# Score operands of a dilated attention kept in two orders, output halves joined by DMA, transposes ahead of scores

## Chip, cores and metric

The kernel runs on one core of a Trainium2 chip. The metric is the device time of one execution in microseconds (us). Three runs of the kernel before took 2604.08, 2596.65 and 2601.12 us, median 2601.12.

## What is computed

One encoder layer on 2048 positions of width 1024. The input is normalised and projected once; half of the mixing width goes to attention (8 heads of 64), half to a gated unit that works in chunks of 128 positions. Attention runs three branches per head, with (window, dilation) of (128, 1), (512, 4) and (2048, 16): each query sees 64 keys on either side at that dilation, and itself.

```python
def dilated_window_branch(q, k, v, rel_bias, window, dil):
    # query at p attends to keys p + dil*j for |j| <= window // (2*dil)
    ...
    s = jnp.einsum('brnqhd,brnkhd->brnhqk', qb, kw).astype(jnp.float32)
    s = s + bias.transpose(2, 0, 1)
    s = jnp.where(valid[:, None], s, NEG_INF)
    m = jnp.max(s, axis=-1, keepdims=True)
    p = jnp.exp(s - m)
    den = jnp.sum(p, axis=-1, keepdims=True)
    o = jnp.einsum('brnhqk,brnkhd->brnqhd', (p / den).astype(v.dtype), vw)
    lse = (m + jnp.log(den))[..., 0].transpose(0, 1, 2, 4, 3)
```

The branches are summed per position with weights in proportion to their softmax denominators. Attention and gated unit go through one output projection, then a feed-forward of width 4096 with squared ReLU follows.

## The kernel before

Every float32 number that TensorE multiplies is split into a high and a low part of a shorter format, and a product is made of three matmuls (high-high, high-low, low-high). The program has three stages.

**The input stage** (0 to 412 us of the trace) normalises and transposes blocks of 512 positions (`prep_all`) and projects them. `do_v` writes values by position to DRAM (`c.vd`), `do_qk` queries and keys by channel (`c.qd`, `c.kd`: high part in [0], low part in [1], 128 channels = two heads each). Four PSUM banks are filled by 96 matmuls; ScalarE and VectorE split each bank into `e2`, and two DMAs of SyncE's queue write the two halves.

**The attention stage** (412 to 1037) goes through 8 heads in 12 steps each: steps 0 to 3 of a head are branch 2 (dilation 16), 4 to 7 branch 1 (dilation 4), 8 to 11 branch 0. A step handles 512 queries; branch 2 has one half step with four blocks of 128 keys, the others have two half steps with two blocks of 192 or 256 keys. Four phases of different heads' steps run together. In step s the program issues the scores and maxima of step s, the exponentials (ScalarE) of s-14, the transposes of s-15, and the values and the gather of s-16. So the values of branch 0 run in steps 0 to 3 of the next head but one.

- `scores`: queries are the stationary operand of 128 columns, with high and low part of the query on the upper and lower 64 partitions of `qs`; keys move, `kl` (low) first, then `ks` (high). For branches 1 and 2 the operands are read from the natural order with a stride of 4 or 16 numbers (`cols`).
- `maxima`: VectorE adds the bias, writes the sum to a tile `p` of a pool of 25 and the negative maximum to `nm`.
- `transposes`, `upper`, `lower`: TensorE turns p into a PSUM tile `t`, ScalarE takes the high part `th`, VectorE the low part `tl`.
- `values`: TensorE, into `o`, a PSUM pool of one buffer. `gather`: branch 2 opens `acc`, branch 1 adds, branch 0 makes `av` (from the pool of p), whose lower 64 partitions (L612) hold the part of the low values. A DMA (L615) brings those to `lo`, GpSimd adds (L619) and writes the head's output `od` (L620).
- `filler`: between these, matmuls of the gated unit (`f`, three at a time, and its transposes), spread by a plan over all steps; the splits `xh` and `xl` that they need are GpSimd's.

TensorE and ScalarE keep the order in which the program is written (`in_order`). The order on VectorE, GpSimd and SyncE is the scheduler's. The loads of the next head are issued in steps 3 to 8 and the values at steps 2, 6 and 10; a paced load waits for the TensorE instruction ahead of it in the program.

**The output stage** (1037 to 1182) and the feed-forward (to the end) are not touched by the change.

## Time and profile before

| | before |
|---|---|
| runs, us | 2604.08, 2596.65, 2601.12 |
| the profiled execution, us | 2600.37 |
| its span, us | 2598.4 |
| TensorE busy | 2451.3 us (94%) |
| VectorE / ScalarE / GpSimd busy | 1053.6 / 942.9 / 431.3 us |
| DMA | 296.13 MB, mean 114 GB/s |

The span is what the trace covers; the rest of the execution lies around it. The clock of TensorE over the span is 0.976 of full. Over the whole program TensorE is the busiest engine, but its share differs by stage: the table of stretches shows where it idles and where its granted clock falls. In rows of the time line the first number is the start, the second the duration, and the bracket tells how long the engine was idle before and what released it.

### The profile page before, as it was taken

How to read it: one execution, taken by the hardware profiler on the slowest of the kernel's cores; microseconds unless marked ns; L12 is line 12 of the kernel's file. 1: busy time of each engine (PE TensorE's matmuls, PEld its weight loads, DVE VectorE, ACT ScalarE, POOL GpSimd, SP SyncE). 2: the span in 40 equal slices, each digit the busy share in tenths (PEclk: the TensorE clock that was granted, in tenths of full speed). 3: DMA queues.
4: the chain of work that ended last, by engine and by line, in shares of the span. 5: the costliest groups of instructions: out<-in, count | busy, mean ns of one | idle time of the engine just before them, and what ended most of it. 6: DMA issues, size and time to landing. Idle time of an engine off the chain costs nothing.

```text
span 2598.4 us, 31362 instructions
## 1 busy us (share of the span) xinstructions
PE 2451.3 (94%) x11591; PEld 2053.8 (79%) x11591; DVE 1053.6 (41%) x2246; ACT 942.9 (36%) x2053; POOL 431.3 (17%) x489
## 2 busy tenths in 40 slices
PE   7999999988898897778999999999999999999998
PEld 6787888877787786557888888888788888888887
DVE  5534523555655554444133223322641332333235
ACT  4424322455665674434322212221533222122212
POOL 4103102322221122322001100110210011001101
PEclk9999999999999998889999999999999999999999
DMA  7644555755665545765121112111431111111113
GB/s 271 217 140 174 171 166 170 197 143 147 172 160 142 138 136 160 212 208 176 33 65 49 49 33 65 49 45 37 157 118 43 55 49 49 41 57 49 49 40 123
DMA packets 208765, 296.13 MB, mean 114 GB/s; under 512 B 37089, under 2 KB 112356, under 8 KB 205540
## 3 DMA queue, kind: packets, MB, share of 16 engines
q1 hardware_dynamic: 202436, 273.15, 35.8%
q10 hardware_dynamic: 4640, 16.79, 1.6%
q0 software_dynamic: 1536, 4.20, 0.6%
q8 instruction: 91, 1.49, 0.2%
q14 instruction: 62, 0.51, 0.1%
HBM read 216.04 MB, written 78.55 MB: 113 GB/s over the span
## 4 chain that ended last, share of the span: by engine, by line
PE 75%; DMA 10%; DVE 6%; issue 4%; POOL 3%; ACT 2%; SPq 1%; POOLq 0%; DVEq 0%; ACTq 0%
PE f L84 11%; PE f L85 11%; PE f L86 11%; PE g L86 8%; PE g L84 8%; PE g L85 8%; PE mm L85 3%; PE mm L86 3%; PE mm L84 3%; DMA fr<-rd 2%; PE s L492 2%; PE s L493 2%; PE t L569 2%; DVE p L505 1%; DMA lo<-av 1%
## 5 line engine op out<-in xcount | busy, mean ns | idle before, releaser
L84 PE MATMUL f<-hl,wh 128*128 128x512 f32 x1024 | 399.2, 390 | 4.7 <-ACT wh L56 4.7
L85 PE MATMUL f<-hh,wl 128*128 128x512 f32 x1024 | 399.2, 390 | 2.9 <-DVE wl L57 2.9
L84 PE MATMUL g<-wl,fh 128*128 128x512 f32 x1024 | 399.0, 390 | 0.0
L86 PE MATMUL f<-hh,wh 128*128 128x512 f32 x1024 | 398.8, 389 | 0.0
L85 PE MATMUL g<-wh,fl 128*128 128x512 f32 x1024 | 398.6, 389 | 0.0
L86 PE MATMUL g<-wh,fh 128*128 128x512 f32 x1024 | 398.5, 389 | 0.0
L56 ACT ACTIVATE wh<-wraw,gain 128x512 fp32r<-128x512 f32 x200 | 143.3, 724 | 502.0 <-PE g L86 423.2
L955 POOL TENSOR_TENSOR sq<-sq 128x512 f32<-128x512 f32 x128 | 132.1, 1052 | 1160.6 <-ACT sq L954 1160.6
L57 DVE SCALAR_TENSOR_TENSOR wl<-wraw,gain,wh 128x512 fp32r<-128x512 f32 x200 | 155.6, 785 | 271.7 <-ACT wh L56 269.1
L60 DVE TENSOR_TENSOR fl<-sq,fh 128x512 fp32r<-128x512 f32 x128 | 99.3, 776 | 394.4 <-ACT fh L59 385.4
L84 PEld LDWEIGHTS f<-hl,wh 128*128 128x128 f32 x1024 | 192.6, 188 | 45.2 <-ACT wh L56 5.1
L85 PEld LDWEIGHTS f<-hh,wl 128*128 128x128 f32 x1024 | 192.6, 188 | 43.3 <-DVE wl L57 3.4
L86 PEld LDWEIGHTS f<-hh,wh 128*128 128x128 f32 x1024 | 192.6, 188 | 40.0
L86 PEld LDWEIGHTS g<-wh,fh 128*128 128x128 f32 x1024 | 192.2, 188 | 39.9
L85 PEld LDWEIGHTS g<-wh,fl 128*128 128x128 f32 x1024 | 192.2, 188 | 39.7
L84 PEld LDWEIGHTS g<-wl,fh 128*128 128x128 f32 x1024 | 192.2, 188 | 39.7
L982 DVE TENSOR_TENSOR acc<-g,acc 128x512 f32<-128x512 f32 x192 | 127.2, 688 | 165.0 <-PE g L86 165.0
L492 PE MATMUL s<-kl,qs 128*128 128x256 f32 (+2 forms) x384 | 144.9, 385 | 48.1 <-DVE nm L505 44.8
L954 ACT ACTIVATE sq<-f 128x512 f32<-128x512 f32 x128 | 74.8, 597 | 289.9 <-PE f L86 282.7
L558 ACT ACTIVATE p<-p,m 128x256 f32<-128x256 f32 (+2 forms) x384 | 173.3, 456 | 4.0 <-DVE m L530 4.0
L505 DVE CUSTOM_DVE_ANT_0 p<-s,bias 128x256 f32<-128x256 f32 (+2 forms) x384 | 120.2, 353 | 127.9 <-PE t L569 71.9
L60 DVE TENSOR_TENSOR wl<-wraw,wh 128x512 fp32r<-128x512 f32 x144 | 100.2, 697 | 172.9 <-ACT wh L59 171.5
(150 smaller groups left out, 4197.6 us busy)
## 6 DMA issues: line engine op xcount, KB each, us to landing
wraw<-in_w_ff_dram SPq DMA_DIRECT2D x256, 256.0 KB, 2.8
wraw<-in_w_in_dram SPq DMA_DIRECT2D x72, 256.0 KB, 2.9
xt<-in_x_dram SPq DMA_DIRECT2D x32, 512.0 KB, 6.5
v<-vd SPq DMA_DIRECT2D x40, 256.0 KB, 6.2
v<-vd SPq DMA_DIRECT2D x8, 1088.0 KB, 7.6
hd<-ht ACTq DMA_DIRECT2D x16, 512.0 KB, 3.7
vd<-vt SPq DMA_DIRECT2D x16, 512.0 KB, 3.1
qd<-e SPq DMA_DIRECT2D x32, 256.0 KB, 2.8
```

Of the source, the lines that this page charges most:

```text
L56: nc.scalar.activation(hi, src, AF.Copy, scale=scale)
L57: nc.vector.scalar_tensor_tensor(lo, src, scale, f32(hi), ALU.mult, ALU.subtract)
L60: nc.vector.tensor_tensor(lo, src, f32(hi), ALU.subtract)
L84: nc.tensor.matmul(out, lhsT=lh, rhs=rl, start=start, stop=False)
L85: nc.tensor.matmul(out, lhsT=ll, rhs=rh, start=False, stop=False)
L86: nc.tensor.matmul(out, lhsT=lh, rhs=rh, start=False, stop=stop)
L492: nc.tensor.matmul(so, lhsT=ql, rhs=kl[:, ksl], start=True, stop=False)
L505: nc.vector.tensor_tensor_reduce(p[:, at + lo:at + hi], so, o.b[:, br * 256 + lo:br * 256 + hi], -1.0, 1e38, ALU.add, ALU.min, o.nm[:, br, ...
L558: nc.scalar.activation(p[:, at + lo:at + hi], p[:, at + lo:at + hi], AF.Exp, bias=o.m[:, br, cc:cc + 1], scale=-1.0, accum_out=o.dn[:, br, ...
L954: nc.scalar.activation(sq, b, AF.Relu)
L955: nc.gpsimd.tensor_tensor(sq, sq, sq, ALU.mult)
L982: nc.vector.tensor_tensor(av, b, av, ALU.add)
```

## The change

Queries and keys are written to DRAM in two orders, `c.q[0]` and `c.k[0]` by position and `c.q[1]` and `c.k[1]` grouped by position modulo 4, each with high and low part side by side. In `do_qk` one DMA of 512 KB replaces two of 256 KB, and beside it GpSimd reorders `e2` into a tile `pq` (which shares its two buffers with `ht`), from which two DMAs of ScalarE's queue write the second order. Values are stored by head instead of by position.

In the attention stage a head has `q4`, `kh4` and `kl4` in the second order (one buffer of q4 and kh4, two of kl4), which serve branches 1 and 2; for branch 2 GpSimd regroups four blocks of queries at a time (`qg`). Branch 0 has chunks of 512 queries and 576 or 640 keys in natural order (`qn`, `nh`, `nl`, three buffers). A table `LOADS` says in which step what is loaded. The gather's `av` has a buffer of its own, and the pool of p has 26. Instead of the copy and the add, SyncE writes the upper half of av to `od`, and a DMA of GpSimd's queue adds the lower half onto it. Within a half step the transposes come before the scores.

```diff
+def qk_load(nc, pool, h, tag, src, e, lo=0, hi=S, bufs=1):
+    t = pool.tile([P, S if bufs == 1 else 512 if e is None else 640], F32R, name=tag, tag=tag, bufs=bufs)
     r = slice((h % 2) * DH, (h % 2) * DH + DH)
+    for half in range(2):
+        part = (half + h) % 2 if e is None else e
+        nc.sync.dma_start(f32(t[half * DH:half * DH + DH, 0:hi - lo]), f32(src[h // 2][r, part, lo:hi]))
+    return t
...
         def do_qk(ws, h, blk, dst, scale):
...
-                nc.sync.dma_start(f32(dst[0][m][:, sl]), f32(eh))
-                nc.sync.dma_start(f32(dst[1][m][:, sl]), f32(el))
+                nc.sync.dma_start(f32(dst[0][m][:, :, sl]), f32(e2))
+                pq = wk.tile([P, 2, 4, P], F32, name="pq", tag="ht")
+                nc.gpsimd.tensor_copy(pq, f32(e2).rearrange("p e (l r) -> p e r l", r=4))
+                for e in range(2):
+                    nc.scalar.dma_start(f32(dst[1][m][:, e].rearrange("p (r l) -> p r l", r=4)[:, :, blk * P:blk * P + P]),
+                                        pq[:, e])
...
-        pp = ctx.enter_context(tc.tile_pool(name="s2p", bufs=25))
+        pp = ctx.enter_context(tc.tile_pool(name="s2p", bufs=26))
...
+        def loadn(o, k):
+            o.qn[k] = qk_load(nc, c.klp, o.h, "qn", c.q[0], None, 512 * k, 512 * k + 512, 3)
+            lo, hi = max(0, 512 * k - 64), min(S, 512 * k + 576)
+            o.kn[k] = lo, [qk_load(nc, c.klp, o.h, ("nh", "nl")[e], c.k[0], e, lo, hi, 3) for e in range(2)]
...
+        def queries(o, br, i):
+            if br == 2:
+                return o.qg[i // 4][:, i % 4]
+            if br == 1:
+                return o.q4[:, i * P:(i + 1) * P]
+            return o.qn[i // 4][:, i % 4 * P:(i % 4 + 1) * P]
+
+        def regroup(o, k):
+            o.qg[k] = c.klp.tile([P, 4, P], F32R, name="qg", tag="qg")
+            nc.gpsimd.tensor_copy(o.qg[k], f32(o.q4).rearrange("p (r l j) -> p j r l", r=4, j=4)[:, k])
+
+        def keys(o, br, i, e, lo, hi):
             if br == 0:
+                at, t = o.kn[i // 4]
+                return t[e][:, lo - at:hi - at]
+            t = o.k4[e].rearrange("p (r l) -> p r l", r=4)
             if br == 1:
+                return t[:, i // 4, lo:hi]
+            return t[:, i % 4].rearrange("p (l j) -> p j l", j=4)[:, i // 4, :]
...
-                av = pp.tile([P, 512], F32, name="av", tag="p")
+                av = wk.tile([P, 512], F32, name="av", tag="av", bufs=1)
                 nc.vector.tensor_tensor(av, ops, o.acc[:, sl], ALU.add)
-                lo = wk.tile([DH, 512], F32, name="lo", tag="lo", bufs=1)
-                nc.sync.dma_start(lo, av[DH:P])
-                later(2 * step + 1 + 1, combine(o, av, lo, sl), ())
-        def combine(o, av, lo, sl):
-            nc.gpsimd.tensor_tensor(lo, lo, av[0:DH], ALU.add)
-            nc.gpsimd.dma_start(c.od[o.h * DH:(o.h + 1) * DH, sl], lo)
+                nc.sync.dma_start(c.od[o.h * DH:(o.h + 1) * DH, sl], av[0:DH])
+                later(2 * step + 1 + 1, combine(o, av, sl), ())
+        def combine(o, av, sl):
+            nc.gpsimd.dma_start(c.od[o.h * DH:(o.h + 1) * DH, sl], av[DH:P], accum_op=ALU.add)
...
+        LOADS = {0: [(loadb, 0, 1), (regroup, 0, 1)], 1: [(regroup, 0, 2)], 2: [(regroup, 0, 3)], 3: [(loadb, 0, 0)],
+                 5: [(loadn, 0, 0)], 6: [(loadn, 0, 1)], 7: [(loadn, 0, 2)],
+                 8: [(load4, 1, None), (load4, 1, 0)], 9: [(loadn, 0, 3), (load4, 1, 1)], 10: [(loadb, 1, 2)],
+                 11: [(regroup, 1, 0)]}
...
             B(exps, 0)
+            T(transposes, 0)
+            T(upper, 0)
+            filler(frac(FR[0]))
             A(scores, 0)
             A(maxima, 0)
-            filler(frac(FR[0]))
-            T(transposes, 0)
-            T(upper, 0)
             filler(frac(FR[1]))
...
-            A(scores, 1)
-            A(maxima, 1)
-            filler(frac(FR[2]))
...
             T(transposes, 1)
             T(upper, 1)
             T(lower, 1)
+            filler(frac(FR[2]))
+            A(scores, 1)
+            A(maxima, 1)
...
-    c.vd = mk("vd", [S + 2 * VPAD, NH, 2 * DH])
-    c.qd = [[mk(f"qd{e}{m}", [P, S]) for m in range(4)] for e in range(2)]
-    c.kd = [[mk(f"kd{e}{m}", [P, S]) for m in range(4)] for e in range(2)]
+    c.vd = mk("vd", [NH, S + 2 * VPAD, 2 * DH])
+    c.q = [[mk(f"q{n}{m}", [P, 2, S]) for m in range(4)] for n in range(2)]
+    c.k = [[mk(f"k{n}{m}", [P, 2, S]) for m in range(4)] for n in range(2)]
```

On TensorE, a half step in a head's middle. Before (s: scores, f: gate, t: transposes, o: values):

```order
L492 MATMUL s<-kl,qs 128x192
L493 MATMUL s<-ks,qs 128x192
L492 MATMUL s<-kl,qs 128x256
L493 MATMUL s<-ks,qs 128x256
L84 MATMUL f_7191<-wl,xh 128x512
L85 MATMUL f_7191<-wh,xl 128x512
L86 MATMUL f_7191<-wh,xh 128x512
L569 MATMUL t<-ident,p 128x128 x4
L84 MATMUL f_7191<-wl,xh 128x512
L85 MATMUL f_7191<-wh,xl 128x512
L86 MATMUL f_7191<-wh,xh 128x512
L597 MATMUL o<-tl,v 128x128
```

and after:

```order
L579 MATMUL t<-ident,p 128x128 x4
L84 MATMUL f_7495<-wl,xh 128x512
L85 MATMUL f_7495<-wh,xl 128x512
L86 MATMUL f_7495<-wh,xh 128x512
L503 MATMUL s<-kl_6987,q_6920 128x192
L503 MATMUL s<-kh_6923,q_6920 128x192
L503 MATMUL s<-kl_6987,q_6920 128x256
L503 MATMUL s<-kh_6923,q_6920 128x256
L84 MATMUL f_7495<-wl,xh 128x512
L85 MATMUL f_7495<-wh,xl 128x512
L86 MATMUL f_7495<-wh,xh 128x512
L607 MATMUL o<-tl,v 128x128
```

The scores stood first, with the transposes six rows behind; now the transposes stand first, and three gate matmuls lie between them and the scores.

On VectorE, around a gather of branch 0 in step 2 of a head. Before:

```order
L505 ISA nm 128x1
L577 TENSOR_TENSOR tl<-t,th 128x512
L612 TENSOR_TENSOR av<-o,acc 128x512
L577 TENSOR_TENSOR tl<-t,th 128x512
L505 ISA p,nm<-s,bias 128x128
L505 ISA nm 128x1
L505 ISA p,nm<-s,bias 128x128
L505 ISA nm 128x1
```

and after:

```order
L587 TENSOR_TENSOR tl<-t,th 128x512 x3
L515 ISA p,nm<-s,bias_5440 128x128
L515 ISA nm 128x1
L622 TENSOR_TENSOR av<-o,acc 128x512
L515 ISA p,nm<-s,bias_5440 128x128
L515 ISA nm 128x1
L515 ISA p,nm<-s,bias_5440 128x128
L515 ISA nm 128x1
```

The gather's add stood between two tl, behind the maxima of its step; now it stands in the middle of a step's maxima.

On GpSimd, the steps behind two heads' gathers. Before:

```order
L619 TENSOR_TENSOR lo<-lo,av 64x512
L620 DMA od<-lo 64x512
L619 TENSOR_TENSOR lo<-lo,av 64x512
L620 DMA od<-lo 64x512
L130 TENSOR_SCALAR xh<-fr 128x512
L131 TENSOR_TENSOR xl<-fr,xh 128x512
L619 TENSOR_TENSOR lo<-lo,av 64x512
```

and after:

```order
L131 TENSOR_TENSOR xl<-fr,xh 128x512
L461 CAST qg<-q_6920 128x512 x2
L130 TENSOR_SCALAR xh<-fr 128x512
L131 TENSOR_TENSOR xl<-fr,xh 128x512
L461 CAST qg<-q_6920 128x512 x2
L628 DMA od<-av 64x512 x4
L130 TENSOR_SCALAR xh<-fr 128x512
L131 TENSOR_TENSOR xl<-fr,xh 128x512
L130 TENSOR_SCALAR xh<-fr 128x512
```

The adds and the writes of od were a pair; now the accumulating DMAs of a head stand in one row with the regrouping copies (qg) and the gate's splits ahead of them.

On ScalarE, in the input stage, the evictions of one call of `do_qk` (e is the high part, u belongs to the gated unit). Before:

```order
L78 ACTIVATE e_1224<-mm_1124 128x512
L78 ACTIVATE e_1229<-mm_1125 128x512
L78 ACTIVATE e_1234<-mm_1126 128x512
L286 ACTIVATE u<-sg,bT 128x4x64 x4
L78 ACTIVATE e_1239<-mm_1127 128x512
L286 ACTIVATE u<-sg,bT 128x4x64 x4
```

and after:

```order
L78 ACTIVATE e_1224<-mm_1124 128x512
L78 ACTIVATE e_1232<-mm_1125 128x512
L78 ACTIVATE e_1240<-mm_1126 128x512
L250 DMA q_72<-pq 128x4x128 x2
L250 DMA q_73<-pq 128x4x128 x2
L78 ACTIVATE e_1248<-mm_1127 128x512
L287 ACTIVATE u<-sg,bT 128x4x64 x2
L250 DMA q_74<-pq 128x4x128 x2
L250 DMA q_75<-pq 128x4x128 x2
L287 ACTIVATE u<-sg,bT 128x4x64 x6
```

Four DMA issues of two each, which wait for GpSimd's copies, now stand between the evictions and the gated unit's activations.

## Rows read from the trace of the kernel before

**Rows 1.** Stretches: busy us (instructions) of each engine, TensorE's granted clock, DMA share, GB/s.

```profile
0.00:412.00 412.00, 391.83 (x1794) 321.10 (x1795) 169.92 (x262) 154.80 (x260) 76.74 (x95) 0.99 0.56 186
412.00:475.50 63.50, 60.63 (x285) 52.27 (x285) 29.42 (x127) 12.14 (x20) 26.31 (x28) 0.97 0.69 193
...
536.30:948.30 412.00, 363.96 (x2139) 327.40 (x2140) 229.93 (x885) 245.41 (x770) 81.16 (x86) 0.94 0.59 149
948.30:1037.00 88.70, 72.53 (x412) 61.59 (x411) 36.72 (x58) 53.35 (x156) 26.95 (x28) 0.88 0.54 153
```

**Rows 2.** Sums over heads 2 to 7: steps 0-4, then 5-7, then 8-11.

```profile
sum 183.60, PE 162.26 PEld 145.82 DVE 95.30 ACT 100.51 POOL 45.50; mean PE 27.04 PEld 24.30 DVE 15.88 ACT 16.75 POOL 7.58
...
sum 100.40, PE 96.64 PEld 88.39 DVE 37.86 ACT 60.28 POOL 26.54; mean PE 16.11 PEld 14.73 DVE 6.31 ACT 10.05 POOL 4.42
...
sum 128.00, PE 105.06 PEld 93.19 DVE 96.77 ACT 84.62 POOL 9.12; mean PE 17.51 PEld 15.53 DVE 16.13 ACT 14.10 POOL 1.52
```

**Rows 3.** Waits in 405 to 1040: us in total, times, longest.

```profile
POOL lo L619 <- DMA lo<-av: 208.4, 31, 23.8
...
DVE p L505 <- PE t L569: 71.9, 53, 4.0
...
PE s L492 <- DVE nm L505: 44.8, 44, 2.7
...
DVE p L502 <- POOL lo L619: 28.1, 6, 5.5
...
DVE p L505 <- POOL lo L619: 23.0, 6, 5.1
DVE p L502 <- PE t L569: 22.2, 19, 2.1
```

**Rows 4.** Time line of TensorE: first score and next matmul, in branches 2, 1, 0.

```profile
430.77 0.27 PE L492 MATMUL s<-kl,qs 128*128 128x128 f32 x1
...
432.38 0.43 PE L84 MATMUL f<-wl,xh 128*128 128x512 f32 x1
...
440.15 0.34 PE L492 MATMUL s<-kl,qs 128*128 128x192 f32 x1
...
441.05 0.42 PE L84 MATMUL f<-wl,xh 128*128 128x512 f32 x1
...
459.35 0.25 PE L492 MATMUL s<-kl,qs 128*128 128x192 f32 x1
...
459.81 0.39 PE L84 MATMUL f<-wl,xh 128*128 128x512 f32 x1
```

**Rows 5.** Time line of GpSimd, then VectorE, in head 5's steps 0 to 3.

```profile
762.82 1.28 POOL L619 TENSOR_TENSOR lo<-lo,av 64x512 f32<-64x512 f32 x1 [5.84 <-DMA lo<-av]
764.40 0.55 POOL L620 DMA_DIRECT2D od<-lo  x1 [0.30 <-POOL lo L619]
...
769.73 1.26 POOL L619 TENSOR_TENSOR lo<-lo,av 64x512 f32<-64x512 f32 x1 [4.78 <-DMA lo<-av]
...
771.87 0.63 POOL L130 TENSOR_SCALAR xh<-fr 128x512 fp32r<-128x512 f32 x1
...
764.13 0.29 DVE L505 CUSTOM_DVE_ANT_0 p<-s,bias 128x128 f32<-128x128 f32 x1 [3.72 <-POOL lo L619]
...
771.07 0.11 DVE L504 MEMSET p<- 128x64 f32 x1 [2.83 <-POOL lo L619]
```

**Rows 6.** Two stretches with the DMA engines busy, columns as in rows 1.

```profile
0.00:50.00 50.00, 36.61 (x170) 29.02 (x171) 26.20 (x33) 24.30 (x42) 23.43 (x30) 1.00 0.81 276
...
491.90:515.30 23.40, 22.54 (x126) 20.31 (x125) 11.91 (x54) 16.36 (x47) 6.06 (x6) 1.00 1.02 240
```

**Rows 7.** DMA issues of 412 to 1037: KB each, median us to landing.

```profile
lo<-av SPq DMA_DIRECT2D x32, 128.0 KB, 2.2
od<-lo POOLq DMA_DIRECT2D x32, 128.0 KB, 3.0
```

**Rows 8.** Lines of GpSimd in 0 to 412.

```profile
L192 POOL TENSOR_TENSOR ht<-hh,hl 128x1024 f32<-128x1024 f32 x16 | 39.0, 2445 | 96.8 <-DVE hl L76 81.1 <-DMA hd<-ht 10.7 <-DMA kd<-e 4.9
```

More of the change, by code (lines that the diff above doesn't have):

```diff
@@ L358, in stage1 @@
         c.wu = wload(1536)
[L359 removed]
+        c.qk = c.fctx.enter_context(tc.tile_pool(name="s2q", bufs=1, side="right"))
         c.fk = c.fctx.enter_context(tc.tile_pool(name="s2fk", bufs=2, side="right"))
@@ L363, in stage1 @@
         c.raw = fload(nc, c, c.unit[1])
-        c.qs, c.ks = qk_tiles(c)
-        for k in range(4):
-            qk_load(nc, c, 0, c.qs, c.ks, k)
+        c.first = [qk_load(nc, c.qk, 0, "q4", c.q[1], None), qk_load(nc, c.qk, 0, "kh4", c.k[1], 0)]
         do_v(w, hs[1], 3)
@@ L392, in stage2, with loadb @@
             pass
-        def bias(h):
-            t = wk.tile([P, 640], F32, name="bias", tag="bias")
-            for br, off, at, n in ((0, 127, 0, 256), (1, 127, 256, 256), (2, 191, 512, 128)):
-                ap = c.bt[h, 0:1, br * 384 + off:br * 384 + off + n]
-                nc.sync.dma_start(t[:, at:at + n], bass.AP(ap.tensor, ap.offset, [[3 * 384, P], [1, n]]))
-            return t
+        def loadb(o, br):
+            off, n = (127, 256) if br < 2 else (191, 128)
+            t = o.b[br] = wk.tile([P, n], F32, name=f"bias{br}", tag=f"bias{br}", bufs=1)
+            ap = c.bt[o.h, 0:1, br * 384 + off:br * 384 + off + n]
+            nc.sync.dma_start(t, bass.AP(ap.tensor, ap.offset, [[3 * 384, P], [1, n]]))
         def paced(f, *args):
@@ L416, in load @@
             o = Head()
-            m, r = h // 2, slice((h % 2) * DH, (h % 2) * DH + DH)
             o.h = h
-            o.qs, o.ks = (c.qs, c.ks) if h == 0 else qk_tiles(c)
-            o.kl = cst.tile([P, S], F32R, name="kl", tag="kl", bufs=2)
+            o.qn, o.kn, o.k4, o.qg, o.b = {}, {}, {}, {}, {}
             o.nm = sm.tile([P, 3, 16], F32, name="nm", tag="nm")
@@ L484, in scores @@
             for br, i, at, wd in blocks(g, w2):
-                q, j = cols(o.qs, br, i)
-                kh, _ = cols(o.ks, br, i)
-                kl, _ = cols(o.kl, br, i)
                 lo, hi, base = window(br, i)
                 so = ps[:, at + lo:at + hi]
-                ql = q[:, j * P:(j + 1) * P]
-                ksl = slice(base + lo, base + hi)
-                nc.tensor.matmul(so, lhsT=ql, rhs=kl[:, ksl], start=True, stop=False)
-                nc.tensor.matmul(so, lhsT=ql, rhs=kh[:, ksl], start=False, stop=True)
+                ql = queries(o, br, i)
+                for e in (1, 0):
+                    nc.tensor.matmul(so, lhsT=ql, rhs=keys(o, br, i, e, base + lo, base + hi), start=e == 1, stop=e == 0)
                 todo.append((br, i, at, lo, hi, so))
@@ L530, in exchange @@
             nc.vector.tensor_tensor(mm, mm, o.nm[:, 2, :], ALU.min)
-            zt = sm.tile([16, P], F32, name="zt", tag="zt")
+            zt = sm.tile([16, P], F32, name="zt", tag="zt", bufs=1)
             z = dr.tile([S], F32, name="z", tag="z")
@@ L725, in stage2 @@
         FR = (0.35, 0.6, 0.85, 1.0)
-        heads[0] = load(0)
-        for k in range(4, 6):
-            heads[0].part(k)
+        heads[0] = o = load(0)
+        o.q4, o.k4[0] = c.first
+        load4(o, 1)
+        regroup(o, 0)
+        loadb(o, 2)
         cost = [0.0] * STEPS
@@ L750, in stage2 @@
                 ha, ga = divmod(sa, NG)
-                if ha + 1 < NH:
-                    if ga == LQ:
-                        heads[ha + 1] = load(ha + 1)
-                    if LQ <= ga < LQ + 6:
-                        paced(heads[ha + 1].part, ga - LQ)
+                if ga == 8 and ha + 1 < NH:
+                    heads[ha + 1] = load(ha + 1)
+                for f, d, *rest_ in LOADS.get(ga, []):
+                    if ha + d < NH:
+                        paced(f, heads[ha + d], *rest_)
             for br in range(3):
@@ L785, in stage2 @@
                 run()
-            A(scores, 1)
-            A(maxima, 1)
-            filler(frac(FR[2]))
-            if ga == NG - 1:
-                later(2 * step + 2, exchange(heads[ha]), (XG, ZG))
             T(transposes, 1)
@@ L793, in stage2 @@
             T(lower, 1)
+            filler(frac(FR[2]))
+            A(scores, 1)
+            A(maxima, 1)
+            if ga == NG - 1:
+                later(2 * step + 2, exchange(heads[ha]), (XG, ZG))
             for run in jobs.pop(2 * step + 1, []):
```

54 lines of the change are left out of this document (18 added, 36 removed).

## The prediction

> **What bounds the kernel now.** I read the table of stretches first, because the change touches two of them and no other. The input stage is a TensorE stage: 391.83 us of its 412 are busy [rows 1]. In the attention stage, 412 to 1037, TensorE is still the engine with most work, but it is neither full nor at full clock: over heads 2 to 7 (412 us, 68.7 a head) it is busy 363.96, at a granted clock of 0.94, and the DMA engines are at 0.59 [rows 1]. The output projection and the feed-forward behind 1037 are left as they were, so nothing is looked for there.
>
> Second, heads 2 to 7 cut into three parts [rows 2]. Steps 0 to 4 of a head take 183.60/6 = 30.6 us (TensorE 27.0), steps 5 to 7 take 16.7 (16.1, so TensorE is the limit), steps 8 to 11 take 21.3 (17.5, with VectorE at 16.1).
>
> Third, the waits [rows 3]. TensorE's own wait is for the scores' PSUM buffer (s<-DVE nm, 44.8 us, 44 times), so VectorE's maxima come late. VectorE is late for two reasons: its output tile p is not free because the transposes that read it have not run (71.9 and 22.2 us), and p is not free because a gather's tile from the same pool is still held by the add on GpSimd (28.1 and 23.0). GpSimd in turn waits 208.4 us for the copy of the lower half.
>
> Fourth, the score matmuls [rows 4]. Eight of branch 2 take from 430.77 to the next matmul at 432.38, 1.61 us; four of branch 1 take 0.90 us; the same four shapes of branch 0, whose operands lie in a row, take 0.46. That is what the stride of the operands costs.
>
> **The change, part by part.**
>
> *Operands in a row.* Branch 1 becomes what branch 0 is: 0.90 - 0.46 = 0.44 us less a half step, eight a head, 3.5 us. Branch 2 gets queries in a row and keys at stride 4 rather than 16. The bounds are 0.46 scaled from 448 to 512 columns, 0.53, and eight times a matmul whose keys have stride 4 and twice as many columns (0.90/4 = 0.225 for about 224), so 0.90 at the half. I take 0.90, the row with that stride: 0.7 less (ends 0.7 and 1.1), four a head, 2.8 us. Together 6.3 us of TensorE's time a head, 2.8 + 0.9 in steps 0 to 4 and 2.6 in steps 5 to 7. In steps 5 to 7 TensorE is the limit, so all 2.6 us are gained.
>
> *Transposes before scores, and 26 buffers of p without the gather in them.* A maximum then finds the buffer that the transposes ahead of it have freed, and the 71.9 + 22.2 us of waits on VectorE go; so does most of the 44.8 on TensorE. The place is steps 8 to 11, where TensorE is idle 21.3 - 17.5 = 3.8 us a head and VectorE has 16.1 us of work in the same stretch [rows 2]. I take 3.0 us a head (ends 0 and 3.8).
>
> *Output halves.* The add on GpSimd (1.28 us) goes; it lay beside other work. In its place stand two DMAs in a chain, and the gather's tile has one buffer: VectorE's add may not start before the earlier accumulate has landed. Queued behind it on VectorE are the maxima and the tl of the transposes, and TensorE's next values wait as well, since their PSUM pool has one bank. The chain of before has the same length class: the adds stand at 762.82 and 769.73, 6.9 us apart, and VectorE is held 3.72 and 2.83 us through it [rows 5]. After: add and issue about 1.2 us, the write 2.2 to 3.0 (lo<-av and od<-lo are the two rows of that size [rows 7]), issue 0.55, the accumulate about 3.0 with no row of its own. That is 7.0 to 7.8, and I take 7.3; ends 5.9 (both at 2.2, issue hidden) and 9.5 (behind loads). Three such gaps stand in steps 0 to 3 and tie TensorE: 21.9 us, and the other two steps of the five take 2 x 27.0/5 less 0.7 and 0.9, 9.2, less the idle part of the clock that comes back, about 8.4. That makes 30.3 against 30.6: what the scores give in steps 0 to 4 the chain takes. I count 0 (ends -4.4 and +6). GpSimd's accumulate can stand behind the regrouping copies, which wait for q4, and the splits xh and xl, which wait for the gates; that is in the upper end.
>
> *Regrouped queries.* Four GpSimd copies of 128x512 a head, between 0.63 us (xh<-fr [rows 5]) and half of 2.445 (128x1024 [rows 8]): 2.5 to 5 us a head beside 81.16/6 = 13.5 of GpSimd [rows 1]. Hidden unless q4 lands late: 0.
>
> *Loads.* Queries, high keys and low keys were read once a head, six times 512 KB; now that is read in order 1, and the natural order comes on top in four chunks: 4 x 256 KB of queries and 2 x (576+640+640+576) columns x 512 B of keys, 3.5 MB a head. Before, 412 x 149 GB/s = 61 MB went at a share of 0.59, which is 253 GB/s at a full share [rows 1]; after, (61 + 21)/253 = 325 us of full share in some 370 us. On the mean that fits. In the bursts it may not: from step 5 to the values of branch 0, the chunks (3.5), order 1 for the next head (3.15), two branches' values (2.1) and some 2 MB for the gates (61/6 less 3.15 of operands and 3.1 of values is about 4 a head, of which seven steps in twelve) are due, 10.8 MB, in 14.1 + 18.3 + 2 = 34.4 us. A full share carried 240/1.02 = 235 GB/s in one stretch and 276/0.81 = 341 in another [rows 6], so 10.8 MB take 32 to 46 us, late by 0 to 11.6. I take the middle rate, 288: 37.5 us, late by 3, because TensorE was 22.54 of 23.40 us busy at a share of 1.02, and because the values' rows get longer (up to 8 KB instead of 512 B). SyncE's issues rise by 24 of about 0.5 us a head and lie beside the rest.
>
> [...]
>
> *Input stage.* Thirty-two 256 KB writes fewer on SyncE; 32 copies of 128x1024 on GpSimd (2.445 us for the nearest row [rows 8], 78 us beside 76.74 of 412) and 64 DMAs from ScalarE's queue, which wait for them. Behind each such DMA on ScalarE stand the next PSUM evictions, and TensorE waits for those. A copy of 2.4 us after the split holds ScalarE for about that long, four PSUM banks cover most of it, and 8 issues of 0.55 us a call are new work for an engine busy 154.80 of 412. I take 1 us for each of the eight calls, +8 (0 to 20).
>
> *Sum.* Heads 2 to 7: -2.6 - 3.0 + 0 + 3 = -2.6 each, -16. Heads 0 and 1 have the scores' gain, no gather chain yet and nearly full clock (0.97 in head 0 [rows 1]): -6.3 each, less some start-up, -11. Behind 948.3 two chains stand with little else on TensorE (72.53 of 88.7 busy [rows 1]); six gaps at about 1 us more than before's, +6 (0 to 15). Input stage +8. Together -13. The profiled execution took 2600.37 us, 0.75 below the median of the runs, so 2587.
>
> **The rivals.** *All transfers in time.* At 341 GB/s nothing is late, and if the chain is 5.9 us, steps 0 to 4 follow TensorE: -2.6 - 3.0 - 4.4 = -10 a head, -60; -11 for heads 0 and 1, 0 for the tail, +3 for the input stage: 2532. For it: waits of TensorE for loads are not among its large ones now, and the rows get longer. Against it: a share of 1.02 has already been reached without the added bytes.
>
> *The DMA engines become the bound (slower).* At 253 GB/s, the mean of the heads, the 10.8 MB take 42.7 us, late by 8.3 a head at branch 0's last chunk and its values; TensorE's order is fixed, so everything stands behind them. -5.6 + 8.3 = +2.7 a head, +16, with -11, +6 and +8 a time of 2619; at 240 GB/s 2633. It turns slower by more than 0.3% when a head is late by more than 6.4 us, at about 265 GB/s. For it: the mean rate of this kernel. Against it: part of that mean was paid for by rows of 512 B that go.
>
> *The order does not free VectorE.* VectorE's order is the scheduler's; if the maxima still find no buffer, or wait behind the gather's add, the 3.0 us stay: +18 to my sum, 2605, no change.
>
> **How the numbers follow.** About 0.3%, 7.8 us, is what a measurement here can tell from no change. My forecast (2565 to 2605) has 0.35, two thirds of it faster; all in time 0.25, faster; DMA-bound 0.28, slower; order without effect 0.12, half the same and half slower. That gives faster 0.48, same 0.21, slower 0.31. The likeliest case alone spans 2565 to 2605; with the two other sides the range is 2535 to 2632.
>
> **What would show it.** Right: score runs of 0.46 in branch 1 and about 0.9 in branch 2; VectorE's waits for t and for GpSimd's add gone from p; gathers about 7 us apart with VectorE waiting for DMA od; some TensorE wait for nh, nl or v in steps 8 to 12; DMA share over 0.8 in the heads. Wrong: TensorE waiting for loads by tens of us, gathers 10 us apart, or an input stage longer by more than 20 us, on the slow side; steps of 4 us in a row on the fast side.

## The result: 4.5% slower

The changed kernel took 2722.34 us (median of four runs, 2705.49 to 2723.15) against 2601.79 for the kernel before; the ratio is 1.0451, with a 95% interval of 1.0407 to 1.0494. The forecast was 2587 with a range of 2535 to 2632, so the time lies outside it and on the other side. The profiled execution has a span of 2721.4 us against 2598.4.

Where the 123 us of the span are, read from the first and last instruction of each kind in both traces:

| stretch | before, us | after, us | difference |
|---|---|---|---|
| input stage, to the first scores | 419.8 | 440.9 | +21.1 |
| heads 0 and 1 | 116.5 | 132.3 | +15.8 |
| heads 2 to 7, to the last scores | 407.0 | 461.2 | +54.2 |
| last scores to last values | 70.8 | 87.9 | +17.1 |
| last values to the output projection's first matmul | 15.8 | 32.9 | +17.1 |
| output projection and feed-forward | 1568.5 | 1566.2 | -2.3 |

The first view is the table of stretches of the changed kernel, cut at those points (columns as in rows 1).

```profile
0.00:440.90 440.90, 401.78 (x1822) 327.77 (x1822) 178.54 (x265) 155.69 (x263) 148.24 (x131) 0.99 0.69 217
440.90:511.40 70.50, 58.64 (x263) 48.21 (x264) 28.85 (x124) 10.31 (x17) 28.91 (x30) 0.82 0.71 195
...
573.20:1034.40 461.20, 337.22 (x2107) 304.70 (x2106) 235.57 (x875) 236.15 (x760) 83.16 (x86) 0.84 0.73 180
1034.40:1122.30 87.90, 69.36 (x404) 59.58 (x403) 31.88 (x57) 50.08 (x156) 14.62 (x16) 0.88 0.50 132
1122.30:1155.20 32.90, 6.75 (x23) 5.08 (x23) 5.54 (x9) 5.91 (x10) 2.88 (x3) 0.60 0.71 198
```

The same heads 2 to 7, to the last scores, in the kernel before:

```profile
536.30:943.30 407.00, 358.96 (x2104) 322.94 (x2105) 225.99 (x871) 241.54 (x757) 81.16 (x86) 0.94 0.59 148
```

Over heads 2 to 7 TensorE is busy 337 us, less than the 359 of the same stretch before, in a stretch that is 54 us longer: it idles 124 us instead of 48, and its granted clock is 0.84 where it was 0.94. A mean of 0.84 over 461 us is about 148 us at a granted clock of 0.50 and the rest at 1.00 (in slices of 0.2 us it is 0.50 in 713 of 2306, 143 us, and 1.00 in 1549); before it was about 49 of 407 (0.50 in 242 of 2035 slices, 48 us). The DMA engines are at 0.73 and 180 GB/s instead of 0.59 and 148. Of the 124 us of idle time 79 lie ahead of values, 29 ahead of scores and 16 ahead of one transpose; of the 48 before, 41 lay ahead of scores.

The second view is the waits from 400 to 1160 (us in all, times, longest), which answer to [rows 3].

```profile
POOL od L628 <- DMA od<-av: 156.9, 24, 17.1
...
PEld o L607 <- issue: 68.2, 22, 9.1
...
DVE av L622 <- DMA od<-av: 52.0, 12, 8.6
...
PE o L607 <- DVE av L622: 37.8, 13, 7.3
...
PE s L503 <- DMA nl<-k: 33.0, 6, 7.8
```

What the change was to remove is gone: VectorE's waits of p for the transposes and TensorE's wait of s for VectorE's maxima are no longer among the large ones. What stands there instead are the gather's chain (TensorE's values, o, wait for av, and av for the DMAs of od) and loads (nl, the low keys of branch 0).

The third view is the time line of TensorE at the scores, as in [rows 4]: branch 2, then branch 1.

```profile
451.27 0.36 PE L503 MATMUL s<-kl,qg 128*128 128x128 f32 x1
...
452.26 0.43 PE L84 MATMUL f<-wl,xh 128*128 128x512 f32 x1
...
459.21 0.34 PE L503 MATMUL s<-kl,q 128*128 128x192 f32 x1
...
459.75 0.40 PE L84 MATMUL f<-wl,xh 128*128 128x512 f32 x1
```

Eight matmuls of branch 2 take 0.99 us (1.61 before), four of branch 1 take 0.54 (0.90), each at a granted clock of 1.00. The steps that wait for nothing are as short as that promises: 3.6 to 4.4 us where they took 4.5 to 5.5. But each head has two places that cost more than all of it. The steps of one head (4), in us from first score to first score:

```
before  5.4  5.5  5.6  6.6  7.4  6.5  4.6  5.5  4.7  4.8  5.0  5.5   67.3
after   4.2  3.7  5.6 10.3 10.6  3.0  4.4  3.3  7.0  4.4 10.9  5.6   72.8
```

In the other heads of 2 to 7 step 2 is the long one, with 12.8 to 14.2 us.

**The gather, steps 2 to 4.** The time line of one gather and the next in head 5:

```profile
816.72 0.69 DVE L622 TENSOR_TENSOR av<-o,acc 128x512 f32<-128x512 f32 x1 [1.51 <-PE o L608]
...
818.42 0.47 SPq L624 DMA_DIRECT2D od<-av  x1
...
822.63 0.88 POOL L628 DMA_DIRECT2D od<-av  x1 [2.84 <-DMA od<-av]
828.63 0.69 DVE L622 TENSOR_TENSOR av<-o,acc 128x512 f32<-128x512 f32 x1 [7.75 <-DMA od<-av]
...
829.37 0.58 PE L607 MATMUL o<-tl,v 128*128 128x256 f32 x1 [6.42 <-DVE av L622]
```

The add (av) ends at 817.4; SyncE issues the first write 1.0 us later; GpSimd's accumulate waits until that has landed and issues at 822.63; the next add starts when the accumulate has landed, at 828.63, and TensorE's next values follow at 829.37, 6.42 us idle. One gap is 11.9 us here; from accumulate to accumulate within a head the mean is 8.3 (6.7 to 10.4). In this stall and behind it the granted clock is lower:

```profile
812.80:822.60 9.80, 9.15 (x72) 8.43 (x70) 5.17 (x25) 5.70 (x18) 3.51 (x4) 1.00 0.61 137
822.60:829.40 6.80, 0.38 (x4) 0.17 (x3) 0.77 (x2) 0.00 (x0) 0.88 (x1) 0.69 0.60 175
829.40:841.00 11.60, 11.20 (x57) 9.60 (x57) 6.06 (x27) 7.45 (x29) 1.62 (x2) 0.74 0.33 72
```

The granted clock is 1.00 ahead of the stall, 0.69 on the mean in it and 0.74 in the 11.6 us behind it, in which TensorE is busy 11.20; in slices of 0.5 us it is 0.50 from 825.5 to 835.0 and 1.00 again from 835.5, so TensorE ran at 0.50 in about half of them. Two matmuls of the gate start 0.43 us apart at 833.04 and 0.23 at 836.23.

**The last chunk, step 10.** TensorE waits at the first scores of step 11, which read chunk 3. The stretches of 5 us ahead of that (columns as in rows 1) and the matmul that ends the wait:

```profile
785.00:790.00 5.00, 2.34 (x17) 1.84 (x16) 2.35 (x11) 1.97 (x8) 0.00 (x0) 1.00 1.00 291
790.00:795.00 5.00, 5.00 (x40) 4.73 (x39) 4.43 (x12) 3.66 (x12) 0.00 (x0) 1.00 1.04 240
795.00:800.00 5.00, 5.00 (x39) 4.49 (x37) 4.89 (x15) 4.33 (x15) 0.90 (x1) 1.00 1.04 224
800.00:805.00 5.00, 0.10 (x1) 0.00 (x0) 1.26 (x4) 1.56 (x7) 1.28 (x2) 0.97 1.03 242
```

```profile
807.16 0.55 PE L503 MATMUL s<-nl,qn 128*128 128x256 f32 x1 [7.07 <-DMA nl<-k]
```

The DMA engines are full for 20 us at 224 to 291 GB/s (249 on the mean), and TensorE stands still in the last 5 of them.

Late loads cost TensorE time in two more places. Head 3 has the longest wait of all: ScalarE, which keeps the program's order, stands 18.8 us at the cast of a weight whose load is late, and the exponentials behind it hold TensorE's next transposes.

```profile
728.21 0.62 ACT L59 CAST wh<-wraw 128x512 fp32r<-128x512 f32 x1 [18.76 <-DMA wraw<-in_w_out_dram]
...
729.33 1.18 PE L579 MATMUL t<-ident,p 128*128 128x128 f32 x4 [16.07 <-ACT p L568]
```

In head 0, steps 7 to 10 take 36 us instead of 17. TensorE waits there for operands of the gated unit, not for a chunk, some 12 us in all; the largest wait is for a split whose input (fr) came late, while the DMA engines stood at 0.97 to 1.01 from 475 to 495. Its granted clock was 0.50 to 0.84 in most of the time from 475 to 511.

```profile
493.69 0.80 PE L84 MATMUL f<-wl,xh 128*128 128x512 f32 x1 [5.15 <-POOL xh L130]
```

### The profile page after: what moved, and what is told of

Same layout as the page of the kernel before. It is cut to its first block, busy times and chain, and to the rows that moved or that the text cites. A ratio compares the mean times of both kernels' runs of the same rounds, so it can differ in the third digit from the quotient of the medians.

```text
span 2721.4 us, 31723 instructions
## 1 busy us (share of the span) xinstructions
PE 2441.4 (90%) x11591; PEld 2042.9 (75%) x11591; DVE 1072.0 (39%) x2246; ACT 934.8 (34%) x2053; POOL 501.5 (18%) x521
## 4 chain that ended last, share of the span: by engine, by line
PE 68%; DMA 17%; DVE 4%; issue 4%; POOL 3%; SPq 2%; ACT 2%; ACTq 0%; POOLq 0%; DVEq 0%
PE f L84 10%; PE f L85 10%; PE f L86 10%; PE g L86 8%; PE g L84 8%; PE g L85 8%; DMA od<-av 3%; PE mm L86 3%; PE mm L84 3%; PE mm L85 3%; DMA v<-vd 2%; DMA r<-part 2%; PE s L503 2%; PE o L607 1%; PE t L579 1%
## 5 line engine op out<-in xcount | busy, mean ns | idle before, releaser
L57 DVE SCALAR_TENSOR_TENSOR wl<-wraw,gain,wh 128x512 fp32r<-128x512 f32 x200 | 162.5, 822 | 256.9 <-ACT wh L56 252.6
L607 PE MATMUL o<-tl,v 128*128 128x128 f32 (+1 forms) x448 | 123.7, 304 | 101.8 <-DVE av L622 37.8
L607 PEld LDWEIGHTS o<-tl,v 128*128 128x128 f32 x448 | 97.2, 217 | 116.8 <-issue 68.2
```

Of the source, the lines that this page charges most:

```text
L57: nc.vector.scalar_tensor_tensor(lo, src, scale, f32(hi), ALU.mult, ALU.subtract)
L607: nc.tensor.matmul(ops[:, so], lhsT=vc, rhs=tl[:, sl], start=z == 0, stop=False)
```

## Experiments

Each is compared with the changed kernel (2722.34) or with the kernel before on the same chip (2598.71 to 2602.73 by batch). The edits to the changed kernel alone (e2, e3, e5, e9, e10) were run once each, and the changed kernel's own four runs lie 18 us apart; so a difference of less than about 20 us in their times shows nothing by itself, and their traces have to. The chain first.

**The halves in two tensors (e2).**

```diff
-                nc.sync.dma_start(c.od[o.h * DH:(o.h + 1) * DH, sl], av[0:DH])
-                later(2 * step + 1 + 1, combine(o, av, sl), ())
+                for e in range(2):
+                    nc.sync.dma_start(c.od[e, o.h * DH:(o.h + 1) * DH, sl], av[e * DH:e * DH + DH])
...
```

The output projection loads both tensors, and GpSimd adds them there.

> The changed kernel without the accumulating DMA: both halves of the gather's tile are written to two tensors by SyncE, and the output projection loads both and GpSimd adds them there (16 adds of 128x512). Chain theory (the gather's one buffer is free only when the accumulate has landed, and TensorE's next values wait for it): the stalls ahead of o in steps 2 to 4 (about 12 us a head) and at the end of the attention stage (about 20 us) go, the last values move from 88 us behind the last scores to 70, and the time falls by 70 to 120 us. Rival (TensorE waits there for loads or for the transposes, and the accumulate only hides it): less than 30 us. The waits for nl in step 10 stay by both.

Measured 2645.69, 77 us less. Steps 0 to 4 of heads 2 to 7 take 25.7 us a head instead of 36.9 (30.6 before), and the last values come 66 us behind the last scores instead of 88. TensorE's wait of o for av from 573 to 1034, 30.3 us in the changed kernel, is 8.1 in this one's list of waits:

```profile
PE s L503 <- DMA nl<-k: 26.1, 4, 7.9
...
PE o L607 <- DVE av L622: 8.1, 6, 2.6
```

The chain theory holds. The waits for nl stay, as both theories had it.

**The accumulate alone, on the kernel before (e7).**

```diff
-                av = pp.tile([P, 512], F32, name="av", tag="p")
+                av = wk.tile([P, 512], F32, name="av", tag="av", bufs=1)
...
-                nc.sync.dma_start(lo, av[DH:P])
+                nc.sync.dma_start(c.od[o.h * DH:(o.h + 1) * DH, sl], av[0:DH])
...
-            nc.gpsimd.tensor_tensor(lo, lo, av[0:DH], ALU.add)
-            nc.gpsimd.dma_start(c.od[o.h * DH:(o.h + 1) * DH, sl], lo)
+            nc.gpsimd.dma_start(c.od[o.h * DH:(o.h + 1) * DH, sl], av[DH:P], accum_op=ALU.add)
```

> The kernel before with one part of the change: the gather's tile in a buffer of its own, its upper half written by SyncE and its lower half added by a DMA of GpSimd's queue; pool of 25 for p alone. Chain theory (TensorE's values are tied to the accumulate): stalls of 3 to 7 us ahead of o in steps 2 to 4 of each head, 20 to 60 us slower than before. Rival (the chain of before is as long, and freeing the pool of p makes up for it, as the prediction had it): within 10 us of before or faster.

Measured 2615.88, ratio 1.0062 (1.0043 to 1.0082): slower by 17 us, a little under the 20 to 60 expected. Step 3 of heads 2 to 7 takes 6.5 to 10.2 us instead of 5.5 to 7.7. From the first scores to the last values this kernel is 30 us longer than before; 16 us of it come back in the gap ahead of the output projection and in that stage, which the edit does not change. Over the same stretch the chain costs 84 us in the changed kernel (e2 against it). The chain itself is no shorter in e7, 8.4 us on the mean from accumulate to accumulate. That it costs less there, because TensorE waits for VectorE anyway and because the edit also frees a buffer of p, fits but was not tested apart.

**The writes of the second order from SyncE (e3).**

```diff
-                    nc.scalar.dma_start(f32(dst[1][m][:, e].rearrange("p (r l) -> p r l", r=4)[:, :, blk * P:blk * P + P]),
+                    nc.sync.dma_start(f32(dst[1][m][:, e].rearrange("p (r l) -> p r l", r=4)[:, :, blk * P:blk * P + P]),
```

> The changed kernel with the 64 writes of the second order issued from SyncE's queue instead of ScalarE's. If ScalarE's evictions behind those DMAs cost the input stage its 21 us, the first scores come 10 to 20 us earlier (421 to 431 instead of 441). If the GpSimd copies and the buffers that they share with the transposes cost it, or weight loads behind the waiting writes on SyncE, the first scores come at 436 or later.

Measured 2702.84, 20 us less; the first scores come at 425.6 instead of 440.9. The other traces bear it out: with this edit (e6 and e12 have it too) the first scores come at 423 to 428, in the runs of the changed kernel without it (e2, e5, e9, e10) at 439 to 442. So 15 of the input stage's 21 us come from DMAs on ScalarE's queue that wait for GpSimd, with evictions behind them. The other 6 are not traced.

**The loads in other steps (e1, e5).**

```diff
-        LOADS = {0: [(loadb, 0, 1), (regroup, 0, 1)], 1: [(regroup, 0, 2)], 2: [(regroup, 0, 3)], 3: [(loadb, 0, 0)],
-                 5: [(loadn, 0, 0)], 6: [(loadn, 0, 1)], 7: [(loadn, 0, 2)],
-                 8: [(load4, 1, None), (load4, 1, 0)], 9: [(loadn, 0, 3), (load4, 1, 1)], 10: [(loadb, 1, 2)],
+        LOADS = {0: [(loadb, 0, 1), (regroup, 0, 1), (loadn, 0, 0)], 1: [(regroup, 0, 2)],
+                 2: [(regroup, 0, 3), (loadn, 0, 1)], 3: [(loadb, 0, 0)], 4: [(loadn, 0, 2)], 5: [(load4, 1, 1)],
+                 8: [(load4, 1, None), (load4, 1, 0)], 9: [(loadn, 0, 3)], 10: [(loadb, 1, 2)],
...
```

> The changed kernel with the same loads in other steps: chunks 0, 1 and 2 of branch 0's operands in steps 0, 2 and 4 instead of 5, 6 and 7, the next head's low keys in step 5 instead of 9. Bytes and instructions are the same. Burst theory (the loads of steps 5 to 10 come in more than the DMA engines carry, about 240 GB/s, and the scores of step 10 wait 6 to 8 us a head for nl): the wait of s for nl (33.0 us in the changed kernel) falls under 8, steps 8 and 10 fall from about 7 and 11 us to 4 to 6, and with the clock that comes back the time falls by 50 to 90 us. Rival (the added bytes are too many wherever they are placed): the wait moves to other steps, and less than 20 us are gained. Steps 2 to 4 keep their stalls before the values by both.

That run took 6097.53 us, with the matmuls of the feed-forward at 828 to 831 ns on the mean instead of 389 or 390; it says nothing of the loads, and the kernel was run again:

> The same kernel as e1, where every matmul of the whole program, the feed-forward too, took about twice its time. Burst theory: the wait of s for nl falls from 33.0 us to under 8, steps 8 and 10 from about 7 and 11 us to 4 to 6, and the time falls by 50 to 90 us against the changed kernel's 2722. Rival (too many bytes wherever they are placed): the wait moves, and less than 20 us are gained.

Measured 2691.26, 31 us less: between the two. Step 8 falls to 3.6 to 4.4 us. But step 10 of heads 0 to 6 is 12.5 to 17.8 us, against 8 to 12 in the changed kernel (21.8 in head 3). In heads 2 to 7 step 4 grows from 5 to 11 us to 12 to 16, and step 2 falls from 13 or 14 to 9 or 10 in five of the six. The wait for nl does not fall:

```profile
PE s L503 <- DMA nl<-k: 44.7, 5, 10.3
```

My expectation had the wrong chunk: the wait is for chunk 3, which waits for chunk 0's buffer and stands in step 9 in both kernels.

**Chunk 3 ahead of the next head (e9).**

```diff
-                 8: [(load4, 1, None), (load4, 1, 0)], 9: [(loadn, 0, 3), (load4, 1, 1)], 10: [(loadb, 1, 2)],
+                 9: [(loadn, 0, 3), (load4, 1, None)], 10: [(load4, 1, 0), (load4, 1, 1), (loadb, 1, 2)],
```

> The changed kernel, chunk 3 of branch 0's operands issued in step 9 ahead of the next head's q4, kh4 and kl4, which go to steps 9 and 10 (before: q4 and kh4 in step 8, ahead of it). The wait of s for nl comes at the first scores of step 11, which read chunk 3. Queue theory (chunk 3 shares the DMA engines with the 3.1 MB issued ahead of and behind it): step 10, which holds that wait, falls from about 11 us to 5. If the engines have room behind it, nothing takes its place and the time falls by 40 to 60 us against 2722; if the bytes are what counts, the wait moves to the next head's first scores or its regrouped queries (kl4 and q4 late by as much) and the time stays within 15 us.

Measured 2709.26, 13 us less, which is inside the changed kernel's own spread. Step 10 falls to 3.6 to 4.4 (11.4 in one head), and step 11 rises to 13 to 20, because TensorE now waits for the next head's keys:

```profile
PE s L503 <- DMA kl<-k: 52.6, 6, 10.1
```

The wait moves with the order of the queue: steps 10 and 11 together take 17 to 30 us in heads 2 to 6, against 15 to 30 in the changed kernel. That is the bytes theory.

**Fewer bytes (e10).**

```diff
-            o.kn[k] = lo, [qk_load(nc, c.klp, o.h, ("nh", "nl")[e], c.k[0], e, lo, hi, 3) for e in range(2)]
+            o.kn[k] = lo, [qk_load(nc, c.klp, o.h, "nh", c.k[0], 0, lo, hi, 3)] * 2
```

> The changed kernel without the loads of branch 0's low keys (the high keys' tile is read twice, so branch 0's scores are not the reference's): 1.25 MB of some 14 MB a head less, 8 DMA issues less, the same matmuls. If the bytes of the burst make chunk 3 late, 1.25 MB at 240 GB/s are 5 us a head: step 10 falls from about 11 to 6 or 7 us and the time by 30 to 50 us. If SyncE's queue or a buffer holds chunk 3, not the bytes, less than 15 us.

Measured 2676.81, 46 us less with 1.25 MB a head less. Heads 2 to 7 are 5.7 us a head shorter, half of it in step 8, and step 10 falls to 7.1 to 9.6 in most heads. Chunk 3 is still late, now with its high keys:

```profile
PE s L503 <- DMA nh<-k: 24.1, 5, 5.8
```

So less to load makes chunk 3 less late. The 8 issues that go with the bytes were not taken away alone; that it is the bytes rests on the engines' share of 1.00 to 1.04 ahead of the wait.

**The three edits together (e6).** The diffs of e1, e2 and e3.

> The changed kernel with the edits of e1, e2 and e3 together. If the gather's chain (77 us in e2), the input stage (20 us in e3) and the load burst are three separate costs, they add up: about 2722 - 77 - 20 - 60 = 2565, and with TensorE's granted clock back above 0.93 in the attention stage down to 2520. If the costs hide one another, so that the load waits grow when the chain goes, 2600 or more.

Measured 2637.79, ratio 1.0159 (1.0132 to 1.0185): the costs hide one another. It is 12 us more than 2722 - 77 - 20 = 2626, the estimate for e2 and e3 without the moved loads. Without the chain, heads 2 to 6 still take 67 to 81 us, with steps 4 and 10 at 12 to 17. In step 4 the gather's next add waits for the plain write of the one ahead (issued at 723.26 in head 4, the add at 729.79), which shares the DMA engines with the moved chunks and the values of branch 2. TensorE's wait of o for av is 36.5 us in heads 2 to 7, more than the 30.3 of the changed kernel.

**The transposes first, alone (e4).** The kernel before with the last part of the change; of its two half steps the first:

```diff
             B(exps, 0)
+            T(transposes, 0)
+            T(upper, 0)
+            filler(frac(FR[0]))
             A(scores, 0)
             A(maxima, 0)
-            filler(frac(FR[0]))
-            T(transposes, 0)
-            T(upper, 0)
             filler(frac(FR[1]))
```

> The kernel before with one part of the change: transposes ahead of the scores in each half step; everything else, the pool of 25 with the gather's tile in it too, as before. If this frees VectorE as predicted, its waits of p for t (94 us) fall under 40, TensorE's wait of s for nm falls from 44.8 to under 20, and the time falls by 15 to 30 us. Rival (the wait moves to the transposes, which then wait for ScalarE's exponentials, or p stays held by the gather): within 8 us of before.

Measured 2555.27, ratio 0.981 (0.9777 to 0.9843): 47 us faster, more than expected. The waits for t and nm that answer to [rows 3] are down, in the list from 405 to 1000:

```profile
DVE p L504 <- POOL lo L619: 37.5, 11, 6.0
...
DVE p L505 <- PE t L569: 20.6, 17, 3.0
PEld s L492 <- DVE nm L505: 17.8, 21, 3.1
...
DVE p L502 <- PE t L569: 13.6, 9, 2.1
...
PE s L492 <- DVE nm L505: 11.7, 10, 2.6
```

VectorE's waits of p for t are 34 us in these rows where they were 94, and TensorE's wait of s for nm is 11.7 where it was 44.8. Heads 2 to 7 take 373.8 us instead of 407, and heads 2 to 6 gain 6, 2, 5, 6 and 6 us. Of the 46 us between the two traces 38 lie ahead of the last values; 12 lie in the output projection and the feed-forward, which the edit does not change, and the gap ahead of them is 5 longer.

**With it, the two tensors and values by head (e8).** The diffs of e4 and e2 on the kernel before, av in a buffer of its own, and

```diff
-    c.vd = mk("vd", [S + 2 * VPAD, NH, 2 * DH])
+    c.vd = mk("vd", [NH, S + 2 * VPAD, 2 * DH])
```

> The kernel before with transposes ahead of the scores (2555 in e4), values by head, and both halves of the gather's tile written to two tensors that the output projection adds; operands and loads as before. If the GpSimd chain still costs in e4 (its VectorE waits 37.5 us for the add), 10 to 40 us less than e4: 2515 to 2545. If not, or if the output projection pays for it, 2555 or more.

Measured 2542.97, ratio 0.9793 (0.9765 to 0.9821): faster than both kernels, and with e11, 1.4 us apart, the fastest of the runs. Up to the last values its trace is 36 us shorter than that of e4. The time is only 12 less, because the gap behind the last values is 15 us longer and the stages behind that take 12 us more, as much as in the kernel before. From 532 to 877 (heads 2 to 7) TensorE is busy 334 of 345 us:

```profile
532.00:877.00 345.00, 334.42 (x2106) 311.40 (x2105) 232.74 (x874) 237.98 (x763) 37.18 (x38) 0.98 0.68 175
877.00:940.00 63.00, 62.69 (x405) 54.86 (x403) 32.47 (x58) 49.69 (x156) 9.56 (x10) 1.00 0.56 163
940.00:975.00 35.00, 5.21 (x25) 3.89 (x23) 6.47 (x13) 5.91 (x10) 2.52 (x2) 0.61 0.72 222
```

The stretch from 940 to 975 is the gap ahead of the output projection, 35 us. Loading its first blocks by another queue did not shorten it (e11):

```diff
-                nc.sync.dma_start(fa, c.od[0][:, sl].rearrange("(k p) s -> p k s", p=P))
+                q = nc.gpsimd if i < 2 else nc.sync
+                q.dma_start(fa, c.od[0][:, sl].rearrange("(k p) s -> p k s", p=P))
...
```

> The kernel of e8 with the first two blocks of the output projection loaded by GpSimd's queue instead of SyncE's. In e8 35 us lie between the last values and the first matmul of the output projection (16 in the kernel before), because SyncE's loads of od stand behind weight loads that wait. If that is the cause, the gap falls to 12 to 18 us and the time to 2518 to 2530; if the last division by the denominators (rd) is late by itself, 2540.

Measured 2544.40, the gap 37 us: GpSimd's load itself waited, until 965, for a DMA that writes the gated unit's last part, so the queue of the load is not the cause. The other traces show the same order. In the changed kernel the first load of od goes out when that last write has landed; in the kernel before it went out at 1010.39, ahead of the last values (the last row):

```profile
1141.88 0.33 SPq L702 DMA_DIRECT2D part<-ot  x1
1143.96 0.38 SPq L882 DMA_DIRECT2D fa<-od  x1
...
1010.39 1.76 SPq L868 DMA_DIRECT2D fa<-od  x3
```

In all runs with a gap of 32 us or more the load comes 2 to 3 us behind the issue of that write, and in the three with a gap of 20 or less (before, e4, e7) it is issued 4 to 13 us ahead of the last values. Why the load has to wait for the write in the one kind and not in the other was not tested.

**No chunks (e12).** The diffs of e2 and e3, and in `loadn`:

```diff
-            o.qn[k] = qk_load(nc, c.klp, o.h, "qn", c.q[0], None, 512 * k, 512 * k + 512, 3)
-            lo, hi = max(0, 512 * k - 64), min(S, 512 * k + 576)
-            o.kn[k] = lo, [qk_load(nc, c.klp, o.h, ("nh", "nl")[e], c.k[0], e, lo, hi, 3) for e in range(2)]
+            if not once:
+                once.append((qk_load(nc, c.klp, o.h, "qn", c.q[0], None, 512, 1024, 3),
+                             [qk_load(nc, c.klp, o.h, ("nh", "nl")[e], c.k[0], e, 448, 1088, 3) for e in range(2)]))
+            o.qn[k] = once[0][0]
+            o.kn[k] = max(0, 512 * k - 64), once[0][1]
```

> The changed kernel with the edits of e2 (two tensors for the halves) and e3 (second order written by SyncE), and the natural-order chunks of branch 0 loaded once for the whole stage instead of four times a head: all heads and blocks read the same chunk, so branch 0's scores are not the reference's; TensorE's work is the same, 3.5 MB a head less are loaded. Bytes theory: what is left of the gap to e8 (2543, strided operands) is the added bytes; heads fall from 65 to 78 us in e2 to 50 to 55, and the time to 2480 to 2530, under e8 by what operands in a row are worth (6.3 us a head, 50 us in all, less the input stage's 6). Rival (operands in a row are worth little once TensorE waits elsewhere, or another cost of the new order remains): 2540 or more.

Measured 2550.10, ratio 0.9803 (0.9783 to 0.9823): the rival's side. Taking 3.5 MB a head away, with the issues that load them, brings the time down by 76 us against the sum of e2 and e3 (2722 - 77 - 20 = 2626, an estimate, since the two were not run alone together), so the added loads were the largest cost that those two leave. Steps 8 to 11 of heads 2 to 7 take 8.9 us a head less than in the changed kernel. But the kernel is not faster than e8, whose operands are strided. Heads 2 to 7 take 345.1 us in both:

```profile
536.90:882.00 345.10, 307.22 (x2105) 280.48 (x2106) 230.82 (x869) 233.65 (x754) 60.85 (x60) 0.91 0.70 180
```

TensorE is busy 27 us less (307 against 334): its scores alone take 40 us less, and the other matmuls, at a clock of 0.91 instead of 0.98, some 13 more. The 27 us are lost again to idle time, 41 us in heads 2 to 7 against 11 in e8, most of it for the next head's keys at a head's first scores, for values, and in one wait of 8 us for exponentials:

```profile
PE s L507 <- DMA kl<-k: 12.3, 5, 3.3
...
PE o L611 <- DMA v<-vd: 9.3, 5, 2.8
```

## Why the prediction was wrong

Two terms that the sum had near nothing cost most, the gather's chain and the loads. Against the traces of both kernels, in us:

| part of the sum | predicted | measured |
|---|---|---|
| heads 2 to 7, steps 0 to 4, a head | 0 | +6.2 |
| steps 5 to 7, a head | -2.6 | -5.3 |
| steps 8 to 11, a head | 0 (-3.0 + 3) | +8.2 |
| heads 0 and 1 together | -11 | +15.8 |
| behind the last scores | +6 | +34 |
| input stage | +8 | +21 |

*Scores, right.* 0.99 and 0.54 us were predicted as 0.90 and 0.46; four times 0.62 and eight times 0.36 are 5.4 us a head for the 6.3 predicted, and by TensorE's busy time on the scores of heads 2 to 7, the first number behind the comma, it is 6.5 (before, then after):

```profile
536.30:943.30 407.00, 138.27 (x575) 118.96 (x576) 89.09 (x286) 0.94 0.59 148
573.20:1034.40 461.20, 99.30 (x575) 88.19 (x576) 92.31 (x288) 0.84 0.73 180
```

That they shorten the kernel is what failed: e12 has them without the added bytes and is no faster than e8, which has not.

*Transposes first, right.* Predicted 3 us a head in steps 8 to 11; alone (e4) it gives 2.5 there, and 1.9 in steps 0 to 4 and 1.3 in steps 5 to 7, which I had not counted.

*The gather's chain, one of the two steps that failed.* I priced one gap at 7.3 and let the chain take what the scores give, 0 in sum, with +6 as the end. It was the end that came: the gap is 8.3 on the mean, and the first one of a head 8.2 to 10.4 in all but the last: in most heads its accumulate lands 5.7 to 6.7 us behind its issue (median of all 3.5), and the write ahead of it waits up to 2.4 us for its turn on SyncE. And I took the length of before's chain as a reason for no change. That length hardly changed: from write to write of od it was 7.6 on the mean. But before, the adds on VectorE ran 4.7 us apart and held VectorE's p through the chain (63 us in all, where TensorE's o waited 3.9 for av), and here the next add and TensorE's next values wait for it. e2 gives its price: 11.1 us a head in steps 0 to 4, and 77 us with the tail.

*Loads, the other step that failed.* I took the middle rate of 288 GB/s and 3 us late a head. Full engines carried 249 GB/s over the 20 us above (291 in the first 5, then 224 to 242), close to the 253 of the rival "the DMA engines become the bound"; TensorE's waits for chunk 3 were 4.4 to 7.8 us in five heads, near its 8.3. Without the chunks (e12) steps 8 to 11 are 8.9 us a head shorter, against the 3 of my sum. I weighed a share of 1.02 with a busy TensorE as evidence of room; chunk 3 came late behind 20 us at 1.00 to 1.04. The longer rows of the values, my other reason for the higher rate, can be seen in their loads of 256 KB, which landed in 5.4 us in the changed kernel and in e8 instead of 6.2 (medians), but not in the rate: over heads 2 to 7, 180 GB/s at a share of 0.73 is 247 at a full share; the kernel before had 253. That late loads would also hold ScalarE (head 3) and the gated unit (head 0) was in no term. From 790 to 800 the 240 and 224 GB/s were carried with loads of 64 partitions almost alone on their way; what set that rate no run here shows.

*Input stage.* 8 predicted with an end at 20; 21 measured, 15 of it ScalarE's queue (e3). The mechanism was named, its size was off: the eight calls cost about 2 us each there, not 1.

*The clock, missing from the sum.* In heads 2 to 7 some 100 us more than before ran at a granted clock of 0.50 (148 against 49). The matmuls other than scores are the same in both kernels: values, transposes and gate were busy 94, 78 and 113 us before and 106, 84 and 118 after, so the lower clock cost about 22 us of work, by this estimate. I counted stalls as idle time only; the rows of the 11.6 us behind one stall show this second part.

*The tail.* +6 was predicted; it is +17 to the last values (gone in e2), and +17 in the gap behind them, which had no term. The gap is 32 to 39 us in the changed kernel and in every run made from it, 35 and 37 in e8 and e11, 20 in e4 and 9 in e7. The accumulate is not its cause, since e7 has it and e2 has not; the load of od behind the gated unit's last write is where it lies.

*Chances and range.* By the shares as they are worded, same has 0.18 and slower 0.34, not 0.21 and 0.31. The range failed because the rivals stood one by one, and even so it left out their own times of 2532 and 2633: chain, loads, input stage and tail all went wrong at once.
